# Forgetting attention with the keys on the partitions, in a fused three-branch layer on one core

## The chip, the cores and the metric

The kernel runs on one core of a Trainium2 chip, in one launch. The metric is device time in microseconds (us): the kernel before takes 3056.06 us, the median of three runs (3052.37 to 3063.42). The engines are named as in the profile: PE is the matrix engine and PEld its weight loads, DVE the vector engine, ACT the scalar engine, POOL the GpSimd engine, SP the engine that issues nearly all DMAs here. Each engine runs its own instructions in a fixed order; between engines there are only semaphores. SBUF is the on-chip memory that all of them read, PSUM the memory that PE writes, in banks of 128 partitions by 512 fp32 values.

## The reference, cut to what matters

All sizes: one sequence of 2048 positions, 1024 channels, fp32. The layer normalises x, projects it with one wide matrix, feeds three branches (forgetting attention, a state-space layer, cross-attention into 256 memory tokens), gates each branch, projects and merges them, and ends with an output projection, the residual and a norm. The change touches the forgetting attention alone: 12 heads of 64 channels, causal, with a running sum of log forget gates F in the logits.

```python
def forgetting_attention(q, k, v, log_f):       # q is scaled by 64 ** -0.5
    F = cumsum(log_f)                            # per head, along the positions
    # for each block of 128 queries:
    s = q_block @ k.T + F[query] - F[key]
    s = where(key <= query, s, -1e30)
    p = softmax(s)                               # over the keys
    out = p @ v
...
y_fox = forgetting_attention(q, k, v, log_f) * silu(gf)
merged = gates0 * (y_fox @ w_proj_fox) + gates1 * (y_s5 @ w_proj_s5) + gates2 * (y_mem @ w_proj_mem)
out = rms_norm(x + merged @ w_out)
```

F of the query is the same for all keys of a row, so a softmax doesn't see it; the kernel adds only minus F of the key ("nf").

## The kernel before, in words

Matrix products in near-fp32 precision are made of three products in the one-pass format fp32r: each operand is split into a high and a low part, and `mm3` (lines 144 to 149) multiplies high by high, high by low and low by high. POOL makes the high part (line 890) and DVE the low part (line 892) of most operands.

The program has three stages in time. **Projection** (until about 1590 us of the span): the projections of x, with the state-space branch and the memory branch as side work. **Attention** (`gen_fox`, 1590 to 2567 us): the forgetting attention, with two fillers that `run` (line 1012) mixes in by a pace: `gen_gl`, the second half of the merge-gate projection (24 weight tiles times two chunks of 512 positions), and `gen_merge0`, the merge of the last chunk of positions. **Merge** (`merge_out`, from 2567 us): the merge of the other three chunks, then the output projection. `gen_fox` yields after each small piece; per yield PACE (0.355) filler pieces of six matrix products are put into the program. A scheduler that works on modelled times then fixes the order of each engine's instructions; on the chip each engine keeps that order and waits for semaphores.

**The attention before.** A unit is one head and one pair of query blocks (256 queries), 96 units in all, head by head. Queries lie on the partitions. `fox_scores`: for each block of 128 queries and each 512 keys two matrix products (lines 751 and 752; 64 high and 64 low rows of k stacked on the 128 partitions, against q high and q low) give scores in PSUM; one DVE instruction (753) adds nf, stores them in SBUF and keeps the row maximum. ACT takes the exponential of a whole row in place and its sum (758), DVE the reciprocal (759), POOL multiplies the row by it (762). `fox_pv`: PE transposes each 128 by 128 tile of probabilities (783), because the keys must lie on the partitions for the product with v; ACT copies the transposed tiles to the high part (786, 791), DVE makes the low part (787, 792), and one product (799) of a stationary tile [v high | v low] with a moving tile [p high | p low] of 512 columns gives all partial products, summed by 802 to 806. The causal mask is added by POOL to the nf of the diagonal tile (739). A unit's `fox_pv` is interleaved with the next unit's `fox_scores`. Keys, v and nf are loaded once per head, by SP.

**PSUM in this stage** (`PS2`): A, three banks for scores, B, three for transposes, C, one for the products with v, F, one for the fillers.

Two other places are used below as price lists, because they hold forms of instruction that the attention before lacks. `s5_pair` multiplies plain fp32 operands: line 626 with 128 output partitions, line 586 with 64, where two products in a row write partitions 0 to 63 and 64 to 127. `gen_glu` (line 877) and `merge_out` (975) add two SBUF tiles of 128x512 on POOL.

## Time and profile before

| what | value |
| --- | --- |
| median of three runs (lowest, highest) | 3056.06 us (3052.37, 3063.42) |
| the profiled execution: device time, span of its core | 3061.56 us, 3059.8 us |
| mean granted TensorE clock | 0.989 of full |
| busy PE, DVE, ACT, POOL | 97%, 62%, 30%, 33% of the span |
| DMA | 396.81 MB, mean 130 GB/s |

How to read it: all durations below come from that one profiled execution. A row of the grouped views gives the line, the engine, the operation, output and input tiles, shapes and count, then busy time, mean duration, and idle time before with what ended it. A row of a line's own view gives minimum, median and maximum of the durations in ns. PE's products overlap: a 512-column product is shown with some 0.4 us, while the next starts 0.23 us after it; for PE the distance from start to start is what a product costs. The row of a stretch of time gives each engine's busy time and its count of instructions.

### The profile page before, as it was taken

What the parts mean: (1) busy time and instruction counts of PE and PEld (TensorE: products, weight loads), DVE (VectorE), ACT (ScalarE), POOL (GpSimd) and SP (SyncE); (2) the same over time, 40 slices, a digit from 0 to 9 for tenths busy, and PEclk for the clock granted to TensorE, in tenths of its full rate; (3) what the DMA queues carried; (4) which work ended last, traced back from release to release, by engine and by line L of the source; (5) the groups of instructions that cost most, each with busy time, mean ns of one, the idle gap of its engine ahead of it and who ended that gap; (6) DMA issues with size and microseconds to landing.
All of it is one profiled execution on the core that took longest, in us unless ns stands there. A gap on an engine that the chain in (4) does not pass through costs nothing.

```text
span 3059.8 us, 43529 instructions
## 1 busy us (share of the span) xinstructions
PE 2973.6 (97%) x14656; PEld 2425.4 (79%) x14656; DVE 1885.2 (62%) x4982; ACT 927.3 (30%) x1881; POOL 1005.5 (33%) x1328
## 2 busy tenths in 40 slices
PE   8999999999999999999999999999999998999999
PEld 7889977777777778888878888888887776777787
DVE  5332489899986763322217777777777776565544
ACT  5102111111112321222216666666666440000011
POOL 0010000000002432122116655556665666555500
PEclk9999999999999999999999999999999999999999
DMA  5343323323335555344353444444444546665431
GB/s 167 107 134 99 102 86 118 115 92 117 128 125 158 174 155 170 118 128 124 116 160 99 128 119 111 121 121 111 114 118 132 147 112 194 182 185 166 160 105 69
DMA packets 283118, 396.81 MB, mean 130 GB/s; under 512 B 83060, under 2 KB 147828, under 8 KB 282884
## 3 DMA queue, kind: packets, MB, share of 16 engines
q1 hardware_dynamic: 275696, 381.39, 41.9%
q10 hardware_dynamic: 7200, 12.66, 1.2%
q8 instruction: 116, 1.90, 0.3%
q14 instruction: 106, 0.87, 0.1%
HBM read 265.51 MB, written 128.42 MB: 129 GB/s over the span
## 4 chain that ended last, share of the span: by engine, by line
PE 80%; DMA 7%; DVE 5%; POOL 3%; issue 3%; ACT 1%; SPq 0%; DVEq 0%; POOLq 0%; ACTq 0%
PE psF L147 10%; PE psF L148 10%; PE psF L149 10%; PE psA L149 8%; PE psA L147 8%; PE psA L148 8%; PE psC L799 5%; PE psB L783 5%; PE psA L751 3%; PE psA L752 3%; PE psC L147 2%; PE psC L149 2%; PE psC L148 2%; PE psB L149 1%; PE psB L147 1%
## 5 line engine op out<-in xcount | busy, mean ns | idle before, releaser
L147 PE MATMUL psF<-hh,whi 128*128 128x512 f32 (+1 forms) x1160 | 468.6, 404 | 6.1 <-ACT ehi L238 3.0
L890 POOL TENSOR_SCALAR whi<-wraw 128x1024 fp32r<-128x1024 f32 (+2 forms) x216 | 207.4, 961 | 797.1 <-PE psA L148 324.6
L149 PE MATMUL psF<-hh,wlo 128*128 128x512 f32 (+1 forms) x1160 | 460.0, 397 | 0.2 <-DVE wlo L892 0.2
L148 PE MATMUL psF<-hl,whi 128*128 128x512 f32 (+1 forms) x1160 | 459.4, 396 | 0.0
L892 DVE TENSOR_TENSOR wlo<-wraw,whi 128x1024 fp32r<-128x1024 f32 (+2 forms) x216 | 265.0, 1228 | 220.7 <-POOL whi L890 197.3
L147 PE MATMUL psA<-hh,whi 128*128 128x512 f32 (+1 forms) x816 | 322.3, 397 | 3.5 <-POOL whi L890 2.9
L148 PE MATMUL psA<-hl,whi 128*128 128x512 f32 (+1 forms) x816 | 323.6, 397 | 0.0
L149 PE MATMUL psA<-hh,wlo 128*128 128x512 f32 (+1 forms) x816 | 321.4, 394 | 0.6 <-DVE wlo L892 0.6
L787 DVE TENSOR_TENSOR Pt<-psB,Pt 128x512 fp32r<-128x512 f32 x336 | 226.3, 685 | 76.6 <-ACT Pt L786 74.2
L799 PE MATMUL psC<-Pt,v 128*128 128x512 f32 x864 | 265.8, 397 | 4.9 <-DVE Pt L787 4.3
L147 PEld LDWEIGHTS psF<-hh,whi 128*128 128x128 f32 x1160 | 219.0, 189 | 52.5 <-ACT ehi L238 3.5
L149 PEld LDWEIGHTS psF<-hh,wlo 128*128 128x128 f32 x1160 | 218.6, 188 | 51.5 <-DVE wlo L892 0.6
L148 PEld LDWEIGHTS psF<-hl,whi 128*128 128x128 f32 x1160 | 219.0, 189 | 45.9 <-issue 0.4
L753 DVE CUSTOM_DVE_ANT_0 P<-psA,nf 128x512 f32<-128x512 f32 (+1 forms) x336 | 201.2, 627 | 46.2 <-PE psA L752 26.4
L786 ACT CAST Pt<-psB 128x512 fp32r<-128x512 f32 x336 | 191.8, 586 | 105.3 <-PE psB L783 59.4
L762 POOL TENSOR_SCALAR P<-P,rd 128x768 f32<-128x768 f32 (+1 forms) x240 | 193.4, 822 | 60.2 <-DVE rd L759 38.6
L751 PE MATMUL psA<-kk,qh 128*128 128x512 f32 (+1 forms) x480 | 184.6, 390 | 6.2 <-DVE mx L753 4.2
L147 PEld LDWEIGHTS psA<-hh,whi 128*128 128x128 f32 x816 | 154.0, 189 | 38.9 <-POOL whi L890 3.6
L149 PEld LDWEIGHTS psA<-hh,wlo 128*128 128x128 f32 x816 | 154.3, 189 | 35.4 <-DVE wlo L892 0.8
L148 PEld LDWEIGHTS psA<-hl,whi 128*128 128x128 f32 x816 | 154.4, 189 | 33.4
L799 PEld LDWEIGHTS psC<-Pt,v 128*128 128x128 f32 x864 | 153.3, 189 | 32.4 <-DVE Pt L787 8.2
L783 PE MATMUL psB<-ident,P 128*128 128x128 f32 x1200 | 176.9, 273 | 0.3 <-POOL P L762 0.2
(343 smaller groups left out, 6192.2 us busy)
## 6 DMA issues: line engine op xcount, KB each, us to landing
wraw<-in_w_in SPq DMA_DIRECT2D x90, 512.0 KB, 4.2
s_gl<-ehi SPq DMA_DIRECT2D x96, 256.0 KB, 2.5
g<-s_gl SPq DMA_DIRECT2D x96, 256.0 KB, 4.8
wraw<-in_w_proj SPq DMA_DIRECT2D x64, 320.0 KB, 2.9
s_vs<-ev_v SPq DMA_DIRECT2D x48, 256.0 KB, 2.7
nf<-s_nf SPq DMA_DIRECT2D x24, 512.0 KB, 6.7
v<-s_vs SPq DMA_DIRECT2D x24, 512.0 KB, 6.5
qh<-s_qh SPq DMA_DIRECT2D x96, 128.0 KB, 3.8
```

Of the source, the lines that this page charges most:

```text
L147: nc.tensor.matmul(out, a[0], b[0], start=first, stop=False)
L148: nc.tensor.matmul(out, a[0], b[1], start=False, stop=False)
L149: nc.tensor.matmul(out, a[1], b[0], start=False, stop=last)
L751: nc.tensor.matmul(ps[:, :wm], q[0][:, qs], kk[:, c0:c0 + wm], start=True, stop=False)
L753: nc.vector.tensor_tensor_reduce(out=pr[:, c * 512:c * 512 + w], in0=ps[:, :w], in1=nf[:, c0:c0 + w], scale=1.0, scalar=-3.0e38, op0=ALU.a ...
L762: nc.gpsimd.tensor_scalar(out=c, in0=c, scalar1=rd, scalar2=0.5, op0=ALU.mult, op1=ALU.mult)
L783: nc.tensor.transpose(ps[:, o:o + 128], P[b][:, kt * 128:(kt + 1) * 128], self.ident)
L786: nc.scalar.copy(hi, psv)
L787: nc.vector.tensor_sub(lo, psv, fl32(hi))
L799: self.pe = nc.tensor.matmul(o, v, m, start=(kt == 0), stop=(kt == 2 * G + 1))
L890: self.nc.gpsimd.tensor_scalar(out=hi, in0=x, scalar1=sc, scalar2=1.0, op0=ALU.mult, op1=ALU.mult)
L892: self.nc.vector.tensor_sub(lo, x, fl32(hi))
```

## The change

The forgetting attention is rewritten, and little else.

- Keys lie on the partitions. A unit is one head and one chunk of 512 queries (48 units), with a score tile of 128 keys by 512 queries for each of the 4(c+1) key tiles up to the diagonal of chunk c. ACT brings a tile from PSUM to SBUF, adding nf as a value per partition (line 740 of the new program), POOL masks the diagonal tiles (742).
- The maximum over the keys is now across partitions: DVE keeps a running elementwise maximum of the stored tiles (745, 747), PE transposes the result (751), DVE reduces it (753), copies it into a broadcast (760) and PE transposes that back to a PSUM tile with one value per query (763).
- `fox_pv`: for each tile DVE adds minus the maximum from PSUM (779), ACT takes the exponential (780), POOL adds the tile to a running sum (784 for the first, 782), PE multiplies by v (794), both in plain fp32; even key tiles write output partitions 0 to 63, odd ones 64 to 127. At the end the running sum goes the same way as the maximum (798, 800, 801, 760, 763), and 803 to 811 join the two halves and apply the gate.
- No probabilities are transposed and none are split into high and low parts.
- Units go chunk by chunk from the last chunk to the first, all heads inside a chunk; keys, v and q are loaded per unit; fillers may use chunk 3 after the first twelve units. The pace is 0.36. PSUM: A two banks, B three, C two, F one.
- v is stored unsplit; nf is kept on the chip, transposed by 16 small PE transposes (299).

```diff
-PB, PBS = 4, 4
-KS = 3
+TB = 26
...
-PACE, LAG = 0.355, 8
+PACE, LAG = 0.36, 8
-PS2 = {"A": 3, "B": 3, "C": 1, "F": 1}
+PS2 = {"A": 2, "B": 3, "C": 2, "F": 1}
...
-        nc.sync.dma_start(out=self.s["nf"], in_=e)
+        pz = self.psB()
+        for t in range(16):
+            nc.tensor.transpose(pz[:, t * H:(t + 1) * H], e[:, t * 128:(t + 1) * 128], self.ident[0:H, 0:H])
+        nc.scalar.copy(self.nf, pz[:, :16 * H].rearrange("p (t h) -> p t h", h=H))
...
+    def fox_scores(self, p, h, c, ld, u):
+        kk, _, q = ld
+        mx = p.tile([128, CW], F32, tag="mx", name="mx", bufs=2)
+        ts = u["T"] = []
+        for kt in range(4 * (c + 1)):
+            j = kt - 4 * c
+            a = max(j, 0) * 128
+            w = min(a, 256)
+            ps = self.psA()
+            ks = slice(kt * 128, (kt + 1) * 128)
+            nc.tensor.matmul(ps[:, w:], kk[:, ks], q[0][:, w:], start=True, stop=False)
+            nc.tensor.matmul(ps[:, w:], kk[:, ks], q[1][:, w:], start=False, stop=True)
+            t = p.tile([128, CW], F32, tag="T", name="T", bufs=TB)
+            nc.scalar.activation(t[:, a:], ps[:, a:], AF.Identity, bias=self.nf[:, kt, h:h + 1])
+            if j >= 0:
+                nc.gpsimd.tensor_add(t[:, a:a + 128], t[:, a:a + 128], self.mask)
+            ts.append((t, a))
+            if kt == 0:
+                nc.vector.tensor_copy(mx, t)
+            else:
+                nc.vector.tensor_max(mx[:, a:], mx[:, a:], t[:, a:])
+            yield
+        pt = self.psB()
+        for b in range(4):
+            nc.tensor.transpose(pt[:, b * 128:(b + 1) * 128], mx[:, b * 128:(b + 1) * 128], self.ident)
+        nm = p.tile([128, 4], F32, tag="nm", name="nm", bufs=2)
+        nc.vector.reduce_max(nm, pt.rearrange("p (b k) -> p b k", b=4), axis=AX.X, negate=True)
+        u["m"] = self.fox_rows(p, nm, 128)
+
+    def fox_rows(self, p, x, n):
+        xb = p.tile([128, 4, 128], F32, tag="xb", name="xb", bufs=2)
+        nc.vector.tensor_copy(xb[:, :, :n], x.unsqueeze(2).to_broadcast([128, 4, n]))
+        ps = self.psB()
+        for b in range(4):
+            nc.tensor.transpose(ps[:n, b * 128:(b + 1) * 128], xb[:, b, :n], self.ident)
+        return ps
+
+    def fox_pv(self, p, h, c, ld, u):
...
+        acc = p.tile([128, CW], F32, tag="acc", name="acc", bufs=2)
+        po = self.psC()
+        for g in range(c + 1):
+            for kt in range(4 * g, 4 * g + 4):
+                t, a = u["T"][kt]
+                nc.vector.tensor_add(t[:, a:], u["m"][:, a:], t[:, a:])
+                nc.scalar.activation(t[:, a:], t[:, a:], AF.Exp)
+                if kt:
+                    nc.gpsimd.tensor_add(acc[:, a:], acc[:, a:], t[:, a:])
+                else:
+                    nc.gpsimd.tensor_copy(acc, t)
+                if kt % 2:
+                    yield
+            first = None
+            for kt in ((1, 0, 3, 2) if c == 0 else range(4 * g + 3, 4 * g - 1, -1)):
+                t, a = u["T"][kt]
+                o = po[64 * (kt % 2):64 * (kt % 2) + 64, a:]
...
+                with self.tc.issue_after(first or self.pe.ins) if first or self.pe else nullcontext():
+                    self.pe = nc.tensor.matmul(o, v[:, kt, :], t[:, a:], start=k0, stop=k1)
+                first = self.pe.ins
+        pt = self.psB()
+        for b in range(4):
+            nc.tensor.transpose(pt[:, b * 128:(b + 1) * 128], acc[:, b * 128:(b + 1) * 128], self.ident)
+        den, rd = (p.tile([128, 4], F32, tag=n, name=n, bufs=2) for n in ("den", "rd"))
+        nc.vector.reduce_sum(den, pt.rearrange("p (b k) -> p b k", b=4), axis=AX.X)
+        nc.vector.reciprocal(rd, den)
+        rb = self.fox_rows(p, rd, DH)
+        nc.vector.scalar_tensor_tensor(out=gf, in0=rb[:DH, :], scalar=0.5, in1=gf, op0=ALU.mult, op1=ALU.mult)
...
+        nc.vector.tensor_add(o, po[0:64, :], o)
+        nc.gpsimd.tensor_mul(o, o, gf)
...
+        seq = [(h, c) for c in range(NC - 1, -1, -1) for h in range(H)]
...
+                if i == 1 and n + 1 < len(seq):
+                    ld[n + 1] = self.fox_load(*seq[n + 1])
...
+            self.ready = n >= H
```

How the instructions stand now, at three places. **DVE, in the middle of chunk 3**, one unit's round; T are the stored score tiles, mx the running maximum, xb the broadcast copies, psB a PSUM bank of a transpose. Before, a piece of the same engine's order in the attention:

```order
L787 TENSOR_TENSOR Pt<-psB,Pt 128x2x256
L757 TENSOR_REDUCE nm<-mx 128x1
L787 TENSOR_TENSOR Pt<-psB,Pt 128x2x256
L803 TENSOR_TENSOR ot<-psC,ot 128x256
L787 TENSOR_TENSOR Pt<-psB,Pt 128x2x256
L759 RECIPROCAL rd<-den 128x1
L753 ISA P,mx<-psA,nf 128x512
```

and now, the end of one unit's round and the start of the next:

```order
L800 TENSOR_REDUCE den<-psB 128x4
L747 TENSOR_TENSOR mx<-mx,T 128x512
L801 RECIPROCAL rd<-den 128x4
L747 TENSOR_TENSOR mx<-mx,T 128x512
L760 COPY xb<-rd 128x4x64
L747 TENSOR_TENSOR mx<-mx,T 128x512 x2
L803 SCALAR_TENSOR_TENSOR gf<-psB,gf 64x512
L753 TENSOR_REDUCE nm<-psB 128x4
L747 TENSOR_TENSOR mx<-mx,T 128x512
L760 COPY xb<-nm 128x512
L747 TENSOR_TENSOR mx<-mx,T 128x512 x2
L779 TENSOR_TENSOR T<-psB,T 128x512 x10
```

The additions of a unit (779) stand together, sixteen in chunk 3 with one maximum among them; after them and before the next reduction (800) stand six or seven of the full-size maxima (747), the three of the small diagonal tiles, the copy 745 and a weight's low part (891). The reduction of a unit's own sum (800) stands ahead of the next unit's maximum (753) and additions. In chunk 2 the round reads alike with twelve additions. In chunk 1 it has eight, and the stretch between 800 and 779 holds a filler's 945 and 891 besides; in chunk 0 it has four and no filler.

**POOL at the same place** (acc is the running sum, whi a filler's weights):

```order
L811 TENSOR_TENSOR oo<-oo,gf 64x512
L784 COPY acc<-T 128x512
L782 TENSOR_TENSOR acc<-acc,T 128x512 x7
L742 TENSOR_TENSOR T<-T,mask 128x128
L782 TENSOR_TENSOR acc<-acc,T 128x512
L742 TENSOR_TENSOR T<-T,mask 128x128
L782 TENSOR_TENSOR acc<-acc,T 128x512 x3
L742 TENSOR_TENSOR T<-T,mask 128x128
L889 TENSOR_SCALAR whi<-wraw 128x1024
L742 TENSOR_TENSOR T<-T,mask 128x128
L782 TENSOR_TENSOR acc<-acc,T 128x512
L782 TENSOR_TENSOR acc<-acc,T 128x384
```

Where POOL scaled rows of probabilities before (762), it now has one addition for every score tile but the first (a copy), with the next unit's four masks and a weight split between them; two smaller additions follow the last row. From chunk 2 on the masks mostly stand behind the additions.

**PE in the last twelve units** (chunk 0):

```order
L763 MATMUL psB<-ident,xb 128x128 x4
L794 MATMUL psC<-T,v 64x384
L794 MATMUL psC<-T,v 64x512
L794 MATMUL psC<-T,v 64x128
L794 MATMUL psC<-T,v 64x256
L798 MATMUL psB<-ident,acc 128x128 x4
L763 MATMUL psB<-ident,xb 64x128 x4
L751 MATMUL psB<-ident,mx 128x128 x4
```

No filler product stands between these rows any more: the last one comes in the first unit of chunk 0 at the latest, and the first product of `merge_out` stands behind the last unit's 763.

More of the change, by code (lines that the diff above doesn't have):

```diff
@@ L1 @@
+from contextlib import nullcontext
 import concourse.bass as bass
@@ L840, in gen_fox @@
             for _ in pv:
-                pass
-            self.ready = prev is not None and prev[0] == H - 1 and prev[2] <= 6
-            prev = (h, hd[h], G, P)
+                yield
+            self.ready = n >= H
+            prev = (h, c, ld.pop(n), u)
         for _ in self.fox_pv(p, *prev):
@@ L1104, in host_arrays @@
     a["ident"] = np.eye(128, dtype=np.float32)
-    a["mask"] = np.where(np.arange(128)[None, :] <= np.arange(128)[:, None], 0.0, NEG).astype(np.float32)
+    a["mask"] = np.where(np.arange(128)[:, None] <= np.arange(128)[None, :], 0.0, NEG).astype(np.float32)
     return a
```

166 lines of the change are left out of this document (46 added, 120 removed).

## The prediction

> **What bounds the kernel now.** I read the page's totals first, then the stretches of the three stages, then the chain of work that ended last, then single lines for prices.
>
> ```profile
> span 3059.8 us, 43529 instructions
> PE 2973.6 (97%) x14656; PEld 2425.4 (79%) x14656; DVE 1885.2 (62%) x4982; ACT 927.3 (30%) x1881; POOL 1005.5 (33%) x1328
> PE 80%; DMA 7%; DVE 5%; POOL 3%; issue 3%; ACT 1%; SPq 0%; DVEq 0%; POOLq 0%; ACTq 0%
> 0.00:1590.00 1590.00, 1563.88 (x7745) 1281.40 (x7746) 902.55 (x2528) 328.43 (x648) 214.46 (x307) 0.99 0.42 129
> 1590.00:2567.00 977.00, 949.64 (x5019) 782.41 (x5019) 714.20 (x2068) 571.29 (x1152) 596.78 (x834) 0.99 0.43 123
> 2567.00:3060.00 493.00, 460.06 (x1895) 361.63 (x1893) 268.49 (x388) 27.57 (x81) 194.25 (x187) 0.97 0.47 147
> ```
>
> PE is busy 97% of the span and is 80% of the chain that ended last (third row). By stage (PE, PEld, DVE, ACT, POOL busy, then clock, DMA share, GB/s) it is the bound in all three. The attention takes 977 us, of which PE is busy 950, DVE 714, POOL 597, ACT 571: before the change nothing there has to be fast except PE. The question is whether that still holds when work leaves PE and lands on the others.
>
> **PE's part.** A product costs its distance from start to start:
>
> ```profile
> 1767.93 0.23 PE psA L752
> 1768.40 0.44 PE psB L783 x4
> 1771.05 1.31 PE psB L783 x12
> 1773.76 1.39 PE psC L799 x6
> 417.38 0.59 PE L626 MATMUL psC<-u,m 128*128 128x256 f32 x2
> 417.81 0.59 PE L627 MATMUL psC<-hs,z 128*128 128x256 f32 x2
> 473.00 1.08 PE L586 MATMUL psC<-u,m1t 128*64 128x256 f32 x8
> 474.01 0.33 PE L550 MATMUL psB<-ident,m1r 128*128 128x128 f32 x1
> ```
>
> A one-pass product of 512 columns is 0.23 us, a transpose 0.11 (1.31 over 12). Plain fp32 is shown as two instructions a product: 256 columns take 0.43 us (417.38 to 417.81), so 512 take 0.86. But where two products write the two halves of the output partitions (586), four of them pass in 1.01 us, 0.25 each: the halves run side by side, and two 512-column products cost about 0.9 together. So the fp32 product with v costs nothing extra: a unit of chunk 3 has six such pairs and two narrower ones, 6 x 0.9 + 1.35 = 6.8 us. Scores stay as many columns as before. Transposes fall from 1632 to 16 a unit, 768. With 54 filler products (12.5), 6.9 of scores and 1.8 of transposes a unit of chunk 3 needs 27.9 us of PE; likewise 21.4 in chunk 2 (42 fillers), 15.0 in chunk 1 (some 30), 4.4 in chunk 0 (none). Twelve of each: 824 us against 950 busy now. PE alone would give back over 100 us.
>
> **What lands on DVE, ACT and POOL.** Nearest rows for the new forms (min/median/max in ns in the rows of one line):
>
> ```profile
> L787 DVE TENSOR_TENSOR Pt<-psB,Pt x336: 665/686/694, 1612.1 to 2505.7; 128x512 fp32r<-128x512 f32 x168
> L892 DVE TENSOR_TENSOR ymg<-yr,ymg x64: 673/1195/2864, 2358.0 to 2791.0; 128x512 fp32r<-128x512 f32 x64
> L877 POOL TENSOR_TENSOR gt<-gh,gl x24: 1275/1292/4032, 943.5 to 1171.8; 128x512 f32<-128x512 f32 x24
> L739 POOL TENSOR_TENSOR nf<-nf,mask x192: 444/461/1455, 1549.5 to 2500.9; 128x128 f32<-128x128 f32 x192
> L890 POOL TENSOR_SCALAR whi<-wraw x216: 714/1046/1987, 10.1 to 2856.3; 128x1024 fp32r<-128x1024 f32 x48, 128x640 fp32r<-128x640 f32 x33, 128x768 fp32r<-128x768 f32 x27
> L890 POOL TENSOR_SCALAR ymg<-yr x64: 607/624/1442, 2357.3 to 2790.1; 128x512 fp32r<-128x512 f32 x64
> L866 ACT ACTIVATE gf<-gf x24: 627/632/637, 936.9 to 1135.5; 128x512 f32<-128x512 f32 x24
> L238 ACT ACTIVATE ehi<-psF,bm x72: 667/689/717, 1275.9 to 2348.3; 128x512 f32<-128x512 f32 x72
> L653 DVE TENSOR_REDUCE mnm<-psB x64: 412/420/426, 1197.2 to 1510.3; 128x1 f32<-128x256 f32 x64
> L759 DVE RECIPROCAL rd<-den 128x1 f32<-128x1 f32 x192 | 30.4, 159 | 55.5 <-ACT P L758 40.1 <-ACT Ps L758 15.2
> ```
>
> The addition of the maximum (779, one operand in PSUM) is like 787: 0.69 us, never over 0.694. The running maximum (747, both operands in SBUF) is like 892: 0.67 at best, 1.2 in the median. An addition on POOL (782) is 1.29 (877), a mask 0.46, the copy 784 about 0.62, a weight split 1.05. Exponential 0.63, evacuation 740 0.69. A reduction over 512 columns I extend from 0.42 for 256 to 0.69. The three narrower additions of a diagonal lie between 0.46 and 1.29, together 2.2.
>
> Why 892 varies:
>
> ```profile
> 2569.37 0.62 POOL L890 TENSOR_SCALAR ymg<-yr 128x512 fp32r<-128x512 f32 x1 [0.75 <-DMA yr<-s_yx]
> 2570.02 0.69 DVE L892 TENSOR_TENSOR ymg<-yr,ymg 128x512 fp32r<-128x512 f32 x1 [0.67 <-POOL ymg L890]
> 2575.20 1.80 POOL L975 TENSOR_TENSOR g<-g 128x512 f32<-128x512 f32 x1
> 2575.77 1.78 DVE L892 TENSOR_TENSOR ymg<-yr,ymg 128x512 fp32r<-128x512 f32 x1
> 2576.97 1.06 POOL L890 TENSOR_SCALAR ymg<-yr 128x512 fp32r<-128x512 f32 x1
> ```
>
> With POOL idle it takes 0.69. The one that starts inside a POOL addition (2575.77) ends at 2577.55, 0.55 after that addition's end (2577.00), and POOL's next instruction, 0.62 alone, takes 1.06. So a DVE instruction with two SBUF operands and a POOL instruction exclude each other: DVE waits out POOL's, then POOL loses 0.44. 787 shows that an operand in PSUM avoids it. [...]
>
> **The round that sets the end.** DVE's order as now built has each unit's reduction of its own sum (800) ahead of the next unit's maximum (753) and additions (779). 800 needs the last POOL addition. So nothing of the next unit's additions, exponentials and POOL sums can start before POOL has finished this unit; they are one ring, not a pipeline. Its length in chunk 3:
> - first addition and exponential: 0.69 + 0.63 = 1.3;
> - POOL: 0.62 + 12 x 1.29 + 2.2, with four masks (1.8) and a split (1.05) between: 21.2. DVE's 16 additions and ACT's 16 exponentials, some 10 us each, lie beside it;
> - between 779 and 800 DVE has six full maxima, three small ones and a weight's low part, which now fall into POOL's run: 6 x 0.44 + 0.6 + 0.9 = 4.1;
> - from POOL's end to the next 779: transposes 0.6, reduction 0.69, reciprocal 0.16, two broadcast copies 0.9, 803 and 753 0.69 each, 3.7 in all; and six maxima that stand between, 4.1: 7.9.
>
> Together 34.5 us, against PE's 27.9. Chunk 2: 1.3 + 14.1 (eight additions, a split, masks behind) + 3.5 + 6.8 (two full and three small maxima and the copy 745 between) = 25.7. Chunk 1: 1.3 + 8.7 + 1.5 + 7.0 (with a filler's 945 and 891) = 18.5. Chunk 0: 1.3 + 2.8 and 0.5 of masks + 0.1 + 5.7 (763 of the reciprocal is no longer covered) = 10.4. Twelve of each: 12 x 89.1 = 1069 us.
>
> A hand-over between engines adds 0.03 us (POOL's end 2569.99, DVE's start 2570.02) up to perhaps 0.1; eight a ring, 48 rings, 12 to 38: I take 20. The first unit has no predecessor: 102 fillers and 24 score pairs, 35 us.
>
> **The rest.** After the ring of the last unit `merge_out` begins cold: its first products need splits of POOL and DVE that exclude each other, 0.62 + 0.55 a tile, sixteen tiles, 19 us; before, they lay beside the last fillers. I take 20, bounds 0 and 30. The merge of chunk 3 is done inside the attention in both, and 493 us remain. In the projection DVE's low parts of v go and 16 small transposes come (2 us), in a stage where PE is busy 1564 of 1590: zero, with up to 9 if PE meets the scan of F unfinished. Loads per head are about 5.75 MB against 5, at a DMA share of 0.43 not a bound; a unit's loads are issued a unit ahead:
>
> ```profile
> v<-s_vs SPq DMA_DIRECT2D x24, 512.0 KB, 6.5
> nf<-s_nf SPq DMA_DIRECT2D x24, 512.0 KB, 6.7
> ```
>
> They land in under 7 us, a ring of chunk 1 to 3 is longer, chunk 0's are a quarter of the size: nothing. v's slot is freed by the products of the unit before, and behind that wait SP holds the fillers' weights and stores; uncovered, 6.5 x 36 units = 230 us at worst.
>
> Sum: 1590 + 1069 + 20 + 35 + 20 + 493 = 3227 us of span. Device time was 1.8 over the span and the median 5.5 under that execution: 3223, I say 3222.
>
> **Rivals.**
> *PE stays the bound, faster.* For it: 97% now, and 824 us of PE work left. It needs the rings to overlap, at least in chunks 1 to 3: 12 x (27.9 + 21.4 + 15.0) = 772, chunk 0 by its ring 125, start 7, the 27 us that PE idles there now: 931, with 20 and 493 3034, median 3030 (0.9% faster); with chunk 0 overlapping too, 70 less. Against it: the order is fixed, and 800 stands ahead of 779. 16%.
> *The rings without exclusion, slower but less.* If 747 gets by beside POOL, 4.1, 3.5, 1.5 and 0.1 go: 110 us less, 3112. Against it the rows at 2575. 17%.
> *Halves not side by side.* If the PSUM halves of 512 columns don't overlap as 586's do, PE needs 34.7 in chunk 3 and 26.1 in chunk 2: as long as the rings, in turn with them; the late products also hold the score tiles. Some 3 us a unit over 24 units and 2 over 12: 3320. The same figure stands for late loads. 9%.
>
> The forecast itself, rings with exclusion: 58%, its own range 3130 to 3320.
>
> **How the numbers follow.** Half a per cent, 15 us, is about what can be told from no change. Faster is most of the first rival, 14%; the same, its slow end, 4%; slower the rest, 82%. To 3040 to 3330 I leave out the faster end (13%) and 6% above.
>
> **What would show it.** In the attention's stretch: PE busy about 75 to 80% instead of 97%, waiting at 798 and 763; 747 with a median over 1.1 us and 782 over 1.5, while 779 stays at 0.69; gaps on DVE before 800 that end with PE's 798, and POOL idle some 8 us a unit until ACT's first exponential. Distance between 784s in chunk 3 34 to 37 us, in chunk 0 10 to 12 with PE mostly idle. Products of 794 in pairs at one start. Wrong would be 784s 28 us apart with PE at 97%, or 747 at 0.7: then the ring or the exclusion falls.

## The result

The changed kernel takes 3388.09 us (median of four runs, 3387.38 to 3392.84), the kernel before 3058.34 us on the same chip: a ratio of 1.108, 95% interval 1.106 to 1.111. The direction was forecast (slower, 82%), the size was not: 166 us more were forecast, 330 were measured, and 3388 lies above the range of 3040 to 3330.

The totals of the profile after, with the granted clock over the span in 40 slices:

```profile
span 3386.3 us, 41325 instructions
PE 3055.4 (90%) x13904; PEld 2271.2 (67%) x13904; DVE 2103.5 (62%) x4262; ACT 928.8 (27%) x1786; POOL 1226.3 (36%) x1316
PEclk9999999999999999999999999999888865899999
```

The stretches of the four chunks, the merge, and the whole attention (busy us of PE, PEld, DVE, ACT, POOL, then clock, DMA share, GB/s):

```profile
1586.00:2128.00 542.00, 468.87 (x1944) 286.61 (x1944) 404.03 (x564) 281.34 (x502) 345.97 (x307) 0.93 0.34 94
2128.00:2480.00 352.00, 286.29 (x1217) 174.04 (x1217) 271.20 (x393) 168.09 (x304) 244.53 (x236) 0.93 0.40 111
2480.00:2750.00 270.00, 196.87 (x817) 120.91 (x816) 197.98 (x299) 97.33 (x192) 178.73 (x202) 0.82 0.40 118
2750.00:2890.00 140.00, 76.30 (x270) 44.11 (x268) 72.13 (x140) 25.40 (x60) 52.14 (x79) 0.60 0.20 55
2890.00:3386.00 496.00, 462.64 (x1903) 364.20 (x1902) 271.44 (x391) 27.58 (x81) 193.02 (x189) 0.96 0.48 147
1586.00:2890.00 1304.00, 1028.32 (x4242) 625.67 (x4243) 945.33 (x1393) 572.15 (x1057) 821.37 (x822) 0.87 0.35 100
```

All of it is in the attention: 1304 us (last row) against 977. The projection (1586 against 1590) and the merge (496 against 493) stand as they were. No engine fills the stage: PE is busy 79% of it, DVE 72%, POOL 63%, ACT 44%.

The start of each unit's sum (784; first and last start stand behind the durations, the last row holds the first eight units of chunk 0):

```profile
L784 POOL COPY acc<-T x12: 609/609/610, 1627.0 to 2042.4; 128x512 f32<-128x512 f32 x12
L784 POOL COPY acc<-T x12: 609/609/610, 2079.3 to 2408.6; 128x512 f32<-128x512 f32 x12
L784 POOL COPY acc<-T x12: 609/609/610, 2438.8 to 2698.0; 128x512 f32<-128x512 f32 x12
L784 POOL COPY acc<-T x8: 602/610/612, 2721.9 to 2811.2; 128x512 f32<-128x512 f32 x8
```

Eleven distances a row, seven in the last: 37.8, 29.9, 23.6 and 12.8 us (12.4 over all of chunk 0), where 34.5, 25.7, 18.5 and 10.4 were summed. I cut each ring where the prediction cut it and averaged over the units of a chunk, from the starts and ends in the trace: head (first addition 779 to the first sum), POOL's run (first sum to the end of the last), tail (that end to the next unit's first addition).

| chunk | head, forecast and measured | POOL's run | tail | ring |
| --- | --- | --- | --- | --- |
| 3 | 1.3, 1.5 | 25.3, 25.5 | 7.9, 10.8 | 34.5, 37.8 |
| 2 | 1.3, 1.6 | 17.6, 17.1 | 6.8, 11.2 | 25.7, 30.0 |
| 1 | 1.3, 1.4 | 10.2, 11.6 | 7.0, 10.6 | 18.5, 23.6 |
| 0 | 1.3, 1.6 | 3.4, 3.7 | 5.7, 7.2 | 10.4, 12.4 |

Twelve of each: the tails were summed 12 x (2.9 + 4.4 + 3.6 + 1.5) = 149 us too short, the runs 17, the heads 11. The 20 us that were set apart for hand-overs lie in these parts now, so 157 us are left, and the spans differ by 159 (3386 against 3227). **One term, the tail, was mis-sized.** The rest of this document asks what it is made of, and whether the ring it belongs to is really what sets the time.

A tail in chunk 3, on DVE (start, duration, line; the run of POOL ended at 1766.99):

```profile
1764.35 3.19 DVE L747 TENSOR_TENSOR mx<-mx,T 128x512 f32<-128x512 f32 x3
1768.00 0.69 DVE L747 TENSOR_TENSOR mx<-mx,T 128x512 f32<-128x512 f32 x1 [0.46 <-ACT ehi L238]
1768.61 0.68 DVE L800 TENSOR_REDUCE den<-psB 128x4 f32<-128x512 f32 x1
...
1770.60 0.29 DVE L760 COPY xb<-rd 128x256 f32<-128x256 f32 x1
1771.02 0.69 DVE L747 TENSOR_TENSOR mx<-mx,T 128x512 f32<-128x512 f32 x1
1771.63 0.67 DVE L803 SCALAR_TENSOR_TENSOR gf<-psB,gf 64x512 f32<-64x512 f32 x1
1772.23 0.67 DVE L753 TENSOR_REDUCE nm<-psB 128x4 f32<-128x512 f32 x1
1772.83 1.38 DVE L747 TENSOR_TENSOR mx<-mx,T 128x512 f32<-128x512 f32 x1
1774.13 0.41 DVE L760 COPY xb<-nm 128x512 f32<-128x512 f32 x1
1774.46 1.48 DVE L747 TENSOR_TENSOR mx<-mx,T 128x512 f32<-128x512 f32 x2
1775.86 1.28 DVE L779 TENSOR_TENSOR T<-psB,T 128x512 f32<-128x512 f32 x2
```

The order is the forecast one: 800, then 753, then 779. But the chain crosses PE three times, between POOL's end and 800, between the copy 760 and 803, and between the second 760 and 779. From event to event these crossings take in the means 2.4, 1.5, 1.1 us in chunk 3, 3.0, 1.6, 1.2 in chunk 2, 3.2, 1.8, 1.5 in chunk 1, 1.2, 0.9, 1.3 in chunk 0. The prediction had 0.6 for the first and let maxima cover the others.

A crossing is not all waiting for PE, because DVE does other work in it. In the tail shown, 800 stands behind a maximum that sat 0.46 us, and 803 and 779 follow maxima without a pause. The starts and ends in the trace also give what DVE does between POOL's end and the next 779 (means in us; forecast idle is the 0.6 for transposes, forecast busy the rest of the tail; each wait is put down to what ended it):

| chunk | DVE busy, forecast and measured | DVE idle, forecast and measured | idle for PE's transposes | for scores not yet in SBUF | for a filler's product or split |
| --- | --- | --- | --- | --- | --- |
| 3 | 7.3, 8.6 | 0.6, 2.2 | 0.9 | 1.1 | 0.0 |
| 2 | 6.2, 8.3 | 0.6, 2.9 | 1.5 | 1.0 | 0.3 |
| 1 | 6.4, 7.5 | 0.6, 3.1 | 1.2 | 0.0 | 1.4 |

In chunk 0 DVE is busy 4.9 us and idle 2.3, of them 1.8 for PE's transposes. So both parts were summed too short. In chunk 3 the maxima alone take 5.6 us of a tail, where six at 4.1 were summed; in chunk 2 they take 3.7, and a filler's low part (891), which the sum had not put there, takes 1.0. Two of the waits, over eleven units of chunk 3 (us in total, times, longest; some of the first kind fall into POOL's run):

```profile
DVE mx L747 <- ACT T L740: 17.7, 10, 3.4
DVE den L800 <- PE psB L798: 9.7, 4, 5.2
```

A first crossing in chunk 2, on PE and DVE (POOL's run ended at 2180.56; merged rows in order of time):

```profile
2180.40 0.39 PE L148 MATMUL psF<-hl,whi 128*128 128x512 f32 x1
2180.64 0.40 PE L149 MATMUL psF<-hh,wlo 128*128 128x512 f32 x1
2180.87 0.40 PE L737 MATMUL psA<-qh,kk 128*128 128x512 f32 x1
...
2181.11 0.39 PE L738 MATMUL psA<-ql,kk 128*128 128x512 f32 x1
2181.34 0.38 PE L798 MATMUL psB<-ident,acc 128*128 128x128 f32 x2
2181.47 0.48 PE L737 MATMUL psA<-qh,kk 128*128 128x512 f32 x1
2181.79 0.39 PE L738 MATMUL psA<-ql,kk 128*128 128x512 f32 x1
2182.02 0.38 PE L798 MATMUL psB<-ident,acc 128*128 128x128 f32 x2
...
2182.44 0.69 DVE L800 TENSOR_REDUCE den<-psB 128x4 f32<-128x512 f32 x1 [1.32 <-PE psB L798]
```

In PE's order, filler products (147 to 149) and scores (737, 738) stand ahead of the four transposes and between them. The sum is ready at 2180.56, the last transposes start 1.46 us later, 800 starts after 1.88, and DVE sits idle for 1.32 of these (1.0 in the mean of chunk 2). A prediction that reads DVE's order and not PE's at the same place can't see this.

### The profile page after: what moved, and what is told of

Read it like the earlier page. It is cut to its first block, busy times and chain, and to the rows that moved or that the text cites. A ratio compares the mean times of both kernels' runs of the same rounds, so it can differ in the third digit from the quotient of the medians.

```text
span 3386.3 us, 41325 instructions
## 1 busy us (share of the span) xinstructions
PE 3055.4 (90%) x13904; PEld 2271.2 (67%) x13904; DVE 2103.5 (62%) x4262; ACT 928.8 (27%) x1786; POOL 1226.3 (36%) x1316
## 5 line engine op out<-in xcount | busy, mean ns | idle before, releaser
L782 POOL TENSOR_TENSOR acc<-acc,T 128x512 f32<-128x512 f32 (+3 forms) x432 | 527.2, 1220 | 26.9
L747 DVE TENSOR_TENSOR mx<-mx,T 128x512 f32<-128x512 f32 (+3 forms) x432 | 402.4, 933 | 132.7 <-ACT T L740 69.1
L794 PE MATMUL psC<-T,v 128*64 128x512 f32 (+2 forms) x960 | 279.0, 686 | 143.8 <-ACT T L780 143.8
L740 ACT ACTIVATE T<-psA,nf 128x512 f32<-128x512 f32 x480 | 282.0, 621 | 361.9 <-PE psA L738 256.6
L780 ACT ACTIVATE T<-T 128x512 f32<-128x512 f32 x480 | 245.3, 562 | 209.6 <-DVE T L779 209.6
L779 DVE TENSOR_TENSOR T<-psB,T 128x512 f32<-128x512 f32 x480 | 253.0, 598 | 6.6 <-PE psB L763 6.1
L794 PEld LDWEIGHTS psC<-T,v 128*64 128x64 f32 x960 | 77.7, 164 | 258.7 <-ACT T L780 170.7
L737 PE MATMUL psA<-qh,kk 128*128 128x512 f32 x480 | 200.1, 420 | 18.7 <-ACT T L740 16.2
L738 PE MATMUL psA<-ql,kk 128*128 128x512 f32 x480 | 177.2, 371 | 0.0
```

Source lines behind the costliest of these rows:

```text
L737: nc.tensor.matmul(ps[:, w:], kk[:, ks], q[0][:, w:], start=True, stop=False)
L740: nc.scalar.activation(t[:, a:], ps[:, a:], AF.Identity, bias=self.nf[:, kt, h:h + 1])
L747: nc.vector.tensor_max(mx[:, a:], mx[:, a:], t[:, a:])
L779: nc.vector.tensor_add(t[:, a:], u["m"][:, a:], t[:, a:])
L780: nc.scalar.activation(t[:, a:], t[:, a:], AF.Exp)
L782: nc.gpsimd.tensor_add(acc[:, a:], acc[:, a:], t[:, a:])
```

## The experiments

Times are medians of timed runs (ratio to the kernel before, with 95% interval). "Units" are mean distances between the first additions of consecutive units, chunks 3, 2, 1, 0; the changed kernel has 37.8, 30.0, 23.6, 12.4.

### Is it the ring, or PE?

One score pass. The low part of q is left out of the scores, so PE has 102 us less to do, summed at full clock (the output loses precision).

```diff
-            nc.tensor.matmul(ps[:, w:], kk[:, ks], q[0][:, w:], start=True, stop=False)
-            nc.tensor.matmul(ps[:, w:], kk[:, ks], q[1][:, w:], start=False, stop=True)
+            nc.tensor.matmul(ps[:, w:], kk[:, ks], q[0][:, w:], start=True, stop=True)
```

> The second score product (low part of q) is left out: PE has 16 x 0.23 = 3.7 us less in a unit of chunk 3, 2.5, 1.6 and 0.7 in the others, and nothing else changes. Ring theory: only the waits of the running maximum for scores in the tail (1.2 us a unit in chunk 3, 1.05 in chunk 2) can shrink, and the first unit: at most 30 us less, 3360 to 3390. Rival (PE is still the bound, at its fp32 products and their waits): 12 x 8.5 = 100 us less, 3290.

Measured 3381.45 us (1.105, 1.103 to 1.107), units 37.0, 30.1, 22.7, 12.1. A hundred microseconds less work for PE buy 7: PE's amount of work isn't what sets the time. (From 1586 to 2890 us its busy time fell by 47 us, from 1028 to 981, as the granted clock went from 0.87 to 0.83.)

Few sums. POOL's running sum begins six tiles before the unit's end.

```diff
-                if kt:
+                if kt > max(4 * c - 2, 0):
                     nc.gpsimd.tensor_add(acc[:, a:], acc[:, a:], t[:, a:])
-                else:
+                elif kt == max(4 * c - 2, 0):
                     nc.gpsimd.tensor_copy(acc, t)
```

> Edit on the changed kernel: POOL's running sum begins six tiles before the end of a unit, so that 10, 6 and 2 of its additions of 1.27 us are left out in units of chunks 3, 2 and 1 (the output is then not the reference's: the denominators are too small); nothing else changes. Ring theory: POOL's run is the larger part of the ring, and without these additions DVE's own work stands in its place (16 additions of the maximum, nine maxima, the tail): 29, 24 and 22 us a unit in place of 37.8, 30.0 and 23.6, 12 x 16 = 195 us less than 3388: about 3195. Rival (POOL's sums lie beside waits of DVE and PE that would be there anyway): less than 50 us.

Measured 3286.32 us (1.075, 1.073 to 1.077), units 32.7, 28.0, 22.8, 12.2. POOL's run is in the ring: without ten additions chunk 3's units are 5.1 us shorter. But 102 us came back, not 195: under the ring lies another bound, near 32 us in chunk 3, where PE's need was summed as 27.9. PE is busy 324 of 346 us of chunk 3 here (1664 to 2010). A bound of this size comes back below; that it is the same one was not tested on this kernel.

Late end. The unit's end (798 to 812) is written into the program inside the next unit, as a function of its own.

```diff
                 first = self.pe.ins
+        u["end"] = (gf, acc, po)
+
+    def fox_end(self, p, h, c, ld, u):
...
         pt = self.psB()
...
                     if next(pv, 0) != 0:
                         yield
+                if old and i == min(2, a - 1):
+                    yield from self.fox_end(p, *old)
```

> Theory (the ring): in the changed kernel a unit costs head 1.5 + POOL's run 25.5 + tail 10.8 = 37.8 us in chunk 3 (30.0, 23.6, 12.4 in chunks 2, 1, 0), because DVE's order puts the reduction of a unit's sum ahead of the next unit's additions. Here the end of a unit (transposes of the sum, reduction, gate) is written into the program inside the next unit, behind its first additions of the maximum; no work is added or left out. Then head and tail no longer stand between two POOL runs, and a unit costs the longer of PE's need (27.9, 21.4, 15.0) and POOL's run (25.5, 17.1, 11.6), in chunk 0 what DVE has to do, some 9: about 12 x (28.5 + 22 + 15.5 + 9) = 900 in place of 1240, so 340 us less than the changed kernel's 3388: 3050, between 3000 and 3110. Rival (the unit is set by PE's fp32 products and their waits, or by POOL and DVE keeping each other off, and the order doesn't matter): within 1% of 3388.

Measured 3266.74 us (1.068, 1.067 to 1.070), units 35.9, 27.1, 21.0, 9.4. On DVE six or seven of the next unit's additions now stand ahead of 800. 121 us came back with no work taken away, so the order is a cause. Chunk 0 does what was expected (9.4). But 340 were expected: chunks 3 to 1 meet the next bound at once. Chunk 3 of this kernel (columns as above):

```profile
1654.00:2054.00 400.00, 347.66 (x1451) 211.80 (x1451) 339.85 (x437) 206.99 (x384) 285.44 (x242) 0.95 0.34 94
```

DVE is now busy 85% of it, against 78% in the changed kernel, part of that the maxima's waits for POOL.

### What does the exclusion cost?

Maximum in PSUM. The running maximum of the full tiles lies in a bank taken from the transposes, so these maxima have one SBUF operand.

```diff
-PS2 = {"A": 2, "B": 3, "C": 2, "F": 1}
+PS2 = {"A": 2, "B": 2, "C": 2, "F": 1, "M": 1}
...
-                nc.vector.tensor_max(mx[:, a:], mx[:, a:], t[:, a:])
+                nc.vector.tensor_max(mp if j < 0 else mx[:, a:], mp if j <= 0 else mx[:, a:], t[:, a:])
```

> The running maximum of the full tiles is kept in PSUM in place of SBUF (transpose and broadcast bank group B gives up one of its three banks for it), so that the 13 full-width maxima of a unit have one SBUF operand only. Exclusion theory: they take 0.69 us everywhere, POOL's additions 1.27 to 1.29 beside them, the POOL run of a unit loses the 4.1, 3.5 and 1.5 us of the prediction (chunks 3, 2, 1), the tail stays: 12 x 9.1 = 110 us less, 3278 (3250 to 3310). Rival (a DVE instruction waits on POOL's for another reason than its operands): the maxima keep a mean near 0.93 and the time stays within 1% of 3388.

Measured 3365.17 us (1.100, 1.098 to 1.102), units 36.0, 30.1, 23.3, 12.4. The maxima, first in the changed kernel, then here (minimum, median, maximum in ns):

```profile
L747 DVE TENSOR_TENSOR mx<-mx,T x432: 272/693/1844, 1593.8 to 2833.6; 128x512 f32<-128x512 f32 x94, 128x384 f32<-128x384 f32 x32, 128x128 f32<-128x128 f32 x10, 128x256 f32<-128x256 f32 x8
```

```profile
L748 DVE TENSOR_TENSOR psM<-psM,T x252: 672/700/700, 1590.5 to 2609.4; 128x512 f32<-128x512 f32 x126
L748 DVE TENSOR_TENSOR mx<-mx,T x144: 270/546/1626, 1615.1 to 2806.6; 128x384 f32<-128x384 f32 x48, 128x256 f32<-128x256 f32 x48, 128x128 f32<-128x128 f32 x48
```

The mechanism holds: with the running maximum in PSUM (one operand and the result) no maximum ever takes longer than 0.700 us, while those that keep both operands in SBUF still go up to 1.626. Its price doesn't hold: 23 us, where the prediction had 110. The sums of a unit of chunk 3 take 18.9 us here and 20.3 in the changed kernel, 1.4 less, not 4.1. Too few maxima meet POOL's additions (over half of the full-size ones of chunk 3, 81 of 140, start between POOL's end and the next 784, where POOL adds nothing), and in the mean an addition of chunk 3 that meets two of DVE's 747, 745 and 891 is lengthened by some 0.34 us, one that meets one by 0.11, not by 0.44. The edit also takes a bank from the transposes, and the first crossing of chunk 2 grows from 3.0 to 4.2 us; so the 23 us are what is left of the gain, and no run removes the exclusion alone.

Both edits.

> Both edits together: the unit's end written behind the next unit's first additions, and the running maximum in PSUM. Ring theory: once the ring is open PE sets the units of chunks 3 to 1 (27.9, 21.4, 15.0), and POOL's shorter run (21.4, 13.6, 10.1) buys little more: 0 to 25 us under the kernel with the late end alone, about 3035. Rival (POOL's run is what remains as the bound, 25.5 in chunk 3): 80 to 110 under it.

Measured 3187.62 us (1.042, 1.040 to 1.044), units 32.0, 25.2, 20.5, 9.7. On top of the late end the same edit is worth 79 us: close to the rival's 80 to 110. What a wait costs depends on what is behind it; by the ring's theory most of it fell, in the closed ring, into time that was waited anyway.

### What is the tail made of?

Maxima behind. Each unit's maxima queue on DVE behind the additions of the unit before, so that in DVE's order none of the full-size ones of chunk 3 is left for the tail. A unit's first additions are also written into the program ahead of the next unit's scores.

```diff
-                nc.vector.tensor_add(t[:, a:], u["m"][:, a:], t[:, a:])
+                self.add = nc.vector.tensor_add(t[:, a:], u["m"][:, a:], t[:, a:])
...
+            with self.tc.issue_after(self.add.ins) if self.add else nullcontext():
+                nc.vector.tensor_max(...)
...
+            if next(pv, 0) != 0:
+                done = 1
+                yield
```

> Edit on the changed kernel: each running maximum of a unit is queued on DVE behind the additions of the unit before, so that in DVE's order no maximum stands between the reduction of a unit's sum and the next unit's additions any more (7.8, 5.6, 2.1 and 2.2 stand there in the changed kernel, chunks 3 to 0, with a busy time of 5.6, 3.7, 1.4, 0.9 us and waits for scores of 1.2 and 1.05 us). Nothing is left out. Theory (these maxima and their waits are what made the tail longer than forecast): the tail falls from 10.8, 11.2, 10.6, 7.2 to about 4.5, 6, 8, 6; POOL's run gets 1 to 2 us longer, since more maxima now fall into it: 12 x (4.8 + 4 + 1.5 + 1) = 135 us less than 3388: 3250, between 3200 and 3300. Rival (the tail is long because PE and DVE come late for other reasons, and a maximum more or less only fills the wait): the waits grow by what the maxima leave, and the time stays within 1% of 3388.

Measured 3372.11 us (1.103, 1.101 to 1.105), units 37.2, 30.1, 23.5, 12.0. In chunk 3 the tail falls from 10.8 to 7.7, but POOL's run rises from 25.5 to 28.0, since the maxima meet it there. In chunks 2 and 1 the tail stays at 9.6 and 9.9 us. DVE now waits 3.7, 3.2 and 2.0 us of a tail for PE's transposes in chunks 3 to 1, where it waited 0.9, 1.5 and 1.2. So the rival has the time right, and most of the reason: the maxima filled waits that are there without them, and in chunk 3 what the tail lost POOL's run took.

No fillers. All fillers are issued behind the last product of the attention (nothing left out).

```diff
-DUE = 6.0
+DUE = 0.0
...
-PACE, LAG = 0.36, 8
+PACE, LAG = 0.0, 8
...
-        for _ in fill:
-            pass
+        while True:
+            with self.tc.issue_after(self.pe.ins):
+                if next(fill, 0) == 0:
+                    break
```

> Edit on the changed kernel: all fillers (gate projection, merge of the last chunk) are issued behind the last product of the attention, so the rings run alone. Nothing is left out. Asked of the trace is the distance between first sums. Theory (the ring's own work makes its length; fillers add a split on POOL, a low part and a gate on DVE): 31, 22, 16, 11.5 us in place of 37.8, 30.0, 23.6, 12.4. Rival (the rings are long because PE runs slow after its waits): without fillers PE waits more and the granted clock falls under 0.8 in the stage, and the rings stay at 36, 28, 22, 12.4 or more. Time: the fillers, 270 pieces of six products at 0.233 us, follow behind: about 1590 + 20 + 970 + 380 + 515 = 3475 by the theory, 3640 by the rival.

Measured 3654.19 us (median of two runs), near the rival's 3640; asked were the distances, here for chunks 3, 2, 1, and behind them the stretch of chunk 3:

```profile
L784 POOL COPY acc<-T x12: 611/611/612, 1604.5 to 2001.3; 128x512 f32<-128x512 f32 x12
L784 POOL COPY acc<-T x12: 611/611/612, 2036.9 to 2317.9; 128x512 f32<-128x512 f32 x12
L784 POOL COPY acc<-T x12: 611/611/612, 2344.4 to 2548.6; 128x512 f32<-128x512 f32 x12
1600.00:2033.00 433.00, 302.39 (x976) 133.47 (x976) 361.87 (x475) 228.54 (x403) 288.65 (x256) 0.73 0.27 68
```

36.1, 25.5 and 18.6 us, and 12.3 in chunk 0. The first crossing falls from 3.0 and 3.2 us to 0.66 and 0.62 in chunks 2 and 1, the tails from 11.2 and 10.6 to 6.5 and 6.9: there the surplus of the tail is the fillers. DVE's work in these tails falls from 8.3 and 7.5 us to 4.9 and 5.0 (no low part, no gate, fewer maxima that come late) and its waits from 2.9 and 3.1 to 1.6 and 1.8; those for PE's transposes do not fall (1.5 and 1.7 us). The rings of 25.5 and 18.6 lie between the two theories. Chunk 3 and chunk 0 are the rival's, 36.1 and 12.3 where it had 36 and 12.4, with the granted clock of chunk 3 at 0.73. There the tail falls to 8.4 from 10.8, but POOL's run is 26.3; in the mean the last transpose starts 0.12 us after POOL's end and 800 only after 2.06, behind late maxima on DVE. Whether the low clock is what keeps this ring long was not tested.

Is it the clock? In chunk 0 it is 0.60, and a crossing there is all PE has to do (the copy's end to 803):

```profile
2792.03 0.29 DVE L760 COPY xb<-rd 128x256 f32<-128x256 f32 x1
...
2792.47 1.03 PE L763 MATMUL psB<-ident,xb 128*64 128x128 f32 x4 [1.42 <-DVE xb L760]
...
2793.54 0.68 DVE L803 SCALAR_TENSOR_TENSOR gf<-psB,gf 64x512 f32<-64x512 f32 x1 [1.22 <-PE psB L763]
```

From the copy's end (2792.32) to 803 pass 1.22 us: 0.15 to the first product, 1.03 for the four transposes, which start 0.21 apart in place of 0.11, and 0.04. Spare transposes were put into chunk 0's waits:

```diff
+    def warm(self, c):
+        if c == 0:
+            for _ in range(12):
+                pd = self.psF()
+                for _ in range(3):
+                    self.nc.tensor.transpose(pd[:, 0:128], self.mask, self.ident)
```

> Edit on the changed kernel: in each unit of chunk 0, 36 spare transposes of the mask (128 columns, 0.11 us at full clock) into the fillers' free bank keep PE busy in its waits; nobody reads them, and the order on DVE stays. Asked: is it PE's lower granted clock (0.60 to 0.61 in that stretch) that makes chunk 0's rings 12.4 us in place of the forecast 10.4? Theory: the clock of the stretch rises over 0.85, the passages of the ring through PE (sum's end to its reduction, reciprocal's broadcast to the gate, maximum's broadcast to the first addition: 1.2, 0.9, 1.25 us) get 0.3 to 0.5 shorter each, the distance falls to 11 to 11.5, and the time by 10 to 15 us, to 3375. Rival (the passages are made of hand-overs that know no clock, or the spare products stand in the way): 12.4 or more, time 3385 to 3400.

Measured 3390.44 us (1.108, 1.106 to 1.110). The stretch in the changed kernel, then here:

```profile
2734.00:2870.00 136.00, 75.74 (x288) 45.49 (x288) 73.27 (x150) 30.90 (x73) 53.85 (x83) 0.61 0.15 41
```

```profile
2734.00:2870.00 136.00, 104.55 (x591) 66.20 (x588) 75.83 (x155) 31.57 (x73) 53.22 (x83) 0.83 0.15 43
```

The clock rises to 0.83, the last crossing gets 0.25 us shorter, the first 0.5 longer behind the spare products, the units take 12.8. The rival holds: either the clock is not what made chunk 0 longer, or it can't be bought back with PE's own queue. The run can't tell the two apart.

Even fill: pace 0.318 in place of 0.36, on the changed kernel and on the one with both edits.

> Edit on the changed kernel: pace 0.318 in place of 0.36, so that the fillers last into chunk 0's units. Theory (PE isn't the bound, a filler costs the ring only its split, low part and gate, wherever it stands): what the rings of chunks 3 to 1 lose, those of chunk 0 get; the clock of that stretch rises from 0.60 to over 0.85; the time stays within 25 us of 3388. Rival (the slow clock of chunk 0's stretch lengthens its rings, or PE's load those of chunks 3 to 1): 40 to 80 us less.

> The same pace in the kernel with the late end and the maximum in PSUM (3188 us), where by its chain of waits PE's products are over two thirds of chunk 3. Theory (there PE is the bound of chunks 3 to 1): PE gets 12% fewer fillers in each of their units, 1.5, 1.2 and 0.8 us, and chunk 0 has room for them: 12 x 3.5 = 42 us less, 3146. Rival (still bound by order and waits): within 15 us of 3188.

Measured 3398.66 us (1.112, 1.110 to 1.114), units 36.7, 28.1, 24.2, 15.7: chunks 3 and 2 get shorter, 1 and 0, into which fillers and the merge of chunk 3 move, longer, and the sum nearly stays, as the ring's theory says (the granted clock from 2750 to 2880 us is 0.75, under the expected 0.85). On the opened kernel 3181.00 us (1.040, 1.039 to 1.042), 7 us, not 42: units 30.6, 23.8, 19.0, 13.6. What PE gets back in three chunks chunk 0 pays. It is the fastest complete version tried, and still 4% slower than the kernel before.

### What is under the ring?

Three edits on the kernel with both edits: few maxima, few sums, both (few maxima: `else` becomes `elif j >= -1` ahead of `tensor_max`).

> Edit on the kernel with the late end and the maximum in PSUM (3188 us, units of 32.0, 25.6, 20.2, 9.5 us): the running maximum is taken over the first tile and the last five (diagonal and the one before) alone, so 10, 6 and 2 maxima of 0.69 us are left out on DVE (in range, the result stays the same function). Theory (with the ring open DVE's queue is the bound, busy 27.3 of 32.0 us in chunk 3): units of 28, 23 and 19.5 us, 12 x 7.3 = 88 us less, 3100. Rival (another queue or the coupling of the queues): within 30 us of 3188.

> Edit on the kernel with the late end and the maximum in PSUM (3188 us): POOL's running sum begins six tiles before the end, 10, 6 and 2 additions of 1.27 us left out (denominators too small, the output is not the reference's). Theory (DVE's queue is the bound with the ring open): within 30 us of 3188. Rival (POOL, busy 23.6 of 32.0 us and run after run with 6.7 us between, is still the bound of the open ring): units of 28, 22 and 19 us, 100 us less.

> Both left out, maxima on DVE and sums on POOL, in the kernel with the late end and the maximum in PSUM (3188 us). What is left is PE's need (27.9, 21.4, 15.0 us a unit). If the length of a unit comes from the coupling of DVE and POOL, each nearly enough, it falls more than the two single edits together: 12 x (3.5 + 3.5 + 3) = 120 us less, about 3070. If PE's queue sets it, it falls no more than the better of the two.

Measured 3172.63, 3164.86 and 3159.00 us (1.038, 1.035, 1.033; each within 0.002): 15, 23 and 29 us off 3188. Chunk 3's units stay between 31.5 and 31.8 us, against 32.0, so neither DVE nor POOL nor their coupling sets an open unit there; chunk 1's fall from 20.5 to 18.5 with few sums. Then PE, but not by its amount of work:

> The second score product (low part of q) is left out of the kernel with the late end and the maximum in PSUM (3188 us). On the changed kernel the same saving of PE's work, 3.7, 2.5, 1.6 and 0.7 us a unit, 102 us in all, bought 7 us, since the ring set the time. Theory: with the ring open PE is the bound of chunks 3 and 2 (PE's products are 79% of the chain there) and half of that of chunk 1: 50 to 90 us less, about 3120. Rival (order and waits still set it): within 20 us of 3188.

3183.37 us (1.041, 1.039 to 1.043): 4 us, which is within the spread of the runs. With one product a score tile still took 0.50 us of PE's queue, with two 0.64. So a score seems to wait for a bank, which the runs with a third one test. The first score product in chunk 3 with few maxima and sums (line 738 in that kernel, and 741 the instruction of ACT that empties the bank; busy us and mean ns, then idle time before it and what ended it):

```profile
L738 PE MATMUL psA<-qh,kk 128*128 128x512 f32 (+2 forms) x160 | 67.0, 422 | 9.5 <-ACT T L741 9.0
```

> The kernel with the late end, the maximum in PSUM and pace 0.318 (3181 us) gets 28 score tiles in place of 26; two units of chunk 3 would need 32. Theory (PE is the bound in chunk 3): within 10 us of 3181. Rival (scores wait for tiles that the sums free): 12 x 1.5 = 18 us less or more.

Not the tiles: 3203.70 us (1.047, 1.045 to 1.049), 23 us slower, which I can't explain.

Three score banks. `PS2` becomes `{"A": 3, "B": 2, "C": 2, "F": 1}`; the maximum goes back to SBUF. On the kernel with few maxima and sums, and on the one with the late end:

> The kernel with the late end and both maxima and sums left out (3159 us, 31.8 us a unit in chunk 3) with three PSUM banks for scores in place of two; the bank for the maximum goes (the few maxima lie in SBUF again). There PE is busy 94% of chunk 3, and a score tile takes 0.26 + 0.365 us from start to start of its two products, where a product without waits takes 0.23; with one product left out it took 0.50. Theory (PE's floor of 32 us in place of the forecast 27.9 is made of waits for a score bank that ACT empties, 0.13 to 0.16 us a tile, 2 to 2.5 us a unit of chunk 3): 29.5, 23, 17.5 us, 12 x 5 = 60 us less: 3100. Rival (it is PE's products and their changes of kind themselves): within 15 us of 3159.

> The kernel with the late end alone (3267 us; nothing left out) with three score banks and two for transposes. Theory: the same 2 to 2.5 us a unit where PE's queue sets it, 40 to 60 us less, 3215. Rival (exclusion of DVE and POOL sets it): within 20 us of 3267.

3117.02 us (1.019, 1.017 to 1.021) against 3159, and 3228.06 us (1.056, 1.053 to 1.059) against 3267. In the first, PE's wait for ACT is gone, and PE is busy 303.95 of 306 us at full clock:

```profile
L737 PE MATMUL psA<-qh,kk 128*128 128x512 f32 (+2 forms) x160 | 63.0, 396 | 0.8 <-ACT T L740 0.8
```

```profile
1654.00:1960.00 306.00, 303.95 (x1392) 196.97 (x1388) 202.85 (x316) 195.49 (x364) 119.39 (x132) 1.00 0.44 120
```

Its units take 28.6 us in chunk 3: that is PE's need, 27.9 in the prediction. The difference to 31.8 is the second part of the change's line on PSUM: scores have two banks where they had three, and ACT, which empties them, has exponentials in its queue. The section on the change names the line, and the prediction priced it nowhere.

> Edit on the changed kernel, one line: three PSUM banks for scores and two for transposes in place of two and three. In the changed kernel a score tile takes PE 0.26 + 0.44 us in chunk 3, 0.23 us more than two products without a wait: 16 x 0.23 = 3.7 us a unit. Theory (the forecast left out that scores have two banks now, so PE, ACT and the maxima come late into the ring): units of 35, 28, 22.5 us in place of 37.8, 30.0, 23.6: 12 x 5.9 = 70 us less, 3318. Rival (the closed ring of POOL's run and its tail sets the time, and a score that comes earlier waits elsewhere): within 25 us of 3388.

3389.98 us (1.109, 1.107 to 1.111), units 37.4, 30.4, 24.0, 12.4. In the closed ring the same bank is worth nothing, though a score tile's 0.26 + 0.44 us on PE fell to 0.24 + 0.32. With the one score pass this is the plainest sign that the ring sets the time.

## Why the prediction was off

**What bounds the kernel now, and that the ring takes PE's place: right.** Two edits on the ring shorten the kernel (few sums 102 us, late end 121); of two that lighten PE alone one gives 7 us and the other nothing. PE is busy 79% of the stage (75 to 80 forecast), POOL idles around its end of a unit, the projection and the merge cost what they did.

**PE's part: right where it could be tested.** The halves run side by side, so the rival on them falls. A group of four fp32 products with v, each two instructions, in chunk 3:

```profile
1742.75 3.68 PE L794 MATMUL psC<-T,v 128*64 128x512 f32 x8 [3.24 <-ACT T L780]
...
1749.77 1.94 PE L794 MATMUL psC<-T,v 128*64 128x512 f32 x8
```

1.94 us for four, the last one's end included: 0.49 each, where 0.45 was forecast. After a wait of 3.24 us the same four take 3.68, nearly twice as long, and products are back at 0.23 us from about 1747. The granted clock was 0.50 from 1740.5 to 1747.2, and 0.99 in the 2.5 us before and the 4.8 us after; what lowers it there, no run shows. That the rings would be shorter with PE kept busy was not shown either: with the spare transposes, put into chunk 0 alone, the clock rose from 0.61 to 0.83, and the units took 12.8 us in place of 12.4. Missing from PE's part were the two score banks, 3.2 us a unit of chunk 3 once the ring is open, nothing while it is closed.

**POOL's run: right in sum, for partly wrong reasons.** 25.3, 17.6, 10.2 and 3.4 against 25.5, 17.1, 11.6 and 3.7: in part this is luck. The exclusion was 1.4 us in chunk 3, not 4.1; in its place POOL pauses 0.08 us between two additions, which wait for the exponential or follow one another through a semaphore, and masks wait for scores that ACT has not stored yet:

```profile
1741.65 10.17 POOL L782 TENSOR_TENSOR acc<-acc,T 128x512 f32<-128x512 f32 x7
1753.17 0.46 POOL L742 TENSOR_TENSOR T<-T,mask 128x128 f32<-128x128 f32 x1 [1.34 <-ACT T L740]
```

So the signs named for the exclusion were wrong: the median of 747 is 0.693 us, not over 1.1, that of 782 1.273, not over 1.5; 779 kept its 0.69, as said. By the prediction's own sign ("747 at 0.7") the exclusion would have fallen, and it had not: 64 of the 140 full-size maxima of chunk 3 meet no instruction of POOL and take 0.69 us, while the others take 1.02 us in the mean when they meet one and 1.30 when they meet two. I took the strength of the exclusion from two rows. The copy 745, with one SBUF tile read and one written, is lengthened too, which no term of the sum holds: the nine that meet no instruction of POOL take 0.409 to 0.427 us, the other 39 take 0.90 us in the mean and up to 1.581:

```profile
L745 DVE COPY mx<-T x48: 408/784/1581, 1587.7 to 2831.4; 128x512 f32<-128x512 f32 x48
```

**The step that failed** is the last of the ring's list: "from POOL's end to the next 779: transposes 0.6, ... 7.9". The 7.9, 6.8, 7.0 and 5.7 us measured 10.8, 11.2, 10.6 and 7.2. The sum counted DVE's instructions and one crossing of PE; there are three, in the means 5.0, 5.8, 6.4 and 3.4 us together, and DVE's other work fills them only in part. Both terms were too small. In chunks 3, 2 and 1 DVE has 1.3, 2.1 and 1.1 us more work in the tail than was summed, and sits idle 2.2, 2.9 and 3.1 us where 0.6 was summed, for scores and a filler's product as well as for transposes. In chunks 2 and 1 the runs name the cause: fillers, on PE's queue and on DVE's (without them the tails are 6.5 and 6.9 us, where 6.8 and 7.0 were forecast; for chunk 1 this is luck, since its 7.0 counted a filler's 945 and 891, which take 2.0 us of a tail in the changed kernel). In chunk 0 a bare crossing is 0.9 to 1.25 us, not 0.6: four transposes, the first one's start and the last one's length, at a granted clock of 0.61. In chunk 3 the 2.9 us are 1.3 of work and 1.6 of waits, but what causes them stays open: fewer fillers, no exclusion, no maxima in the tail and a third score bank each move the ring by 0.4 to 1.8 us, and what one leaves another takes.

The chances: the forecast had 58% and its own range to 3320; the case that came was its mechanism with a longer tail. The 6% left above 3330 should have held the uncertainty of a term that no row of the trace before showed, and that came 48 times: 1 us more a tail is 48 us.

**No version beat the kernel before.** With the ring opened, the exclusion removed and the fill evened out the new scheme takes 3181 us; with maxima and sums largely left out and three score banks, 3117.

## To carry to other kernels

Where a chain goes round several engines, sum it with each engine's order at the place where the chain enters its queue: what the scheduler put ahead of and between four transposes costs more than the transposes (the first crossing of chunk 2 took 3.0 us, and 0.66 without fillers), and a term of a microsecond that comes 48 times decides the forecast. A wait has no price of its own: the maximum in PSUM was worth 23 us in the closed ring and 79 in the open one, a third score bank nothing and 39, so price an edit against what stands behind it, and test by giving the supposed bound more room rather than by taking work off it. When no engine fills the stage (PE, the busiest here, 79%) and single edits that should help barely do (six here moved the time by less than 1%), look for an order that closes a ring, and open it first.

## Not expected of the hardware

An fp32 maximum of 128x512 with one operand in PSUM took 0.672 to 0.700 us in all 252 cases; with both in SBUF up to 1.844. A bare crossing from DVE over four PE transposes back to DVE took 0.9 to 1.25 us at a granted clock of 0.61. And raising that clock to 0.83 with spare transposes brought nothing: units of 12.8 us in place of 12.4.
